# A conv-and-attention block on one core: its front, its third weight chunk and its last 512 columns rearranged

## The chip, the cores and the metric

The kernel runs on 1 core of one Trainium2 chip. The metric is device time in microseconds (us). Before the change the median of 3 runs was 740.27 us (739.8 to 740.4). The engines: TensorE (PE in the profile, its weight loads PEld), VectorE (DVE), ScalarE (ACT), GpSimd (POOL, all but unused here) and SyncE (SP), whose queue issues every transfer of this kernel before the change.

## The reference, cut to what matters

One layer over x (512 tokens by 1024), with a condition vector c for x and a vector c_ctx for 256 context tokens:

```python
sh, sc, gt = split(silu(c) @ w_mod + b_mod, 3)             # condition, 3 x 1024
h  = rmsnorm(x, pre_g) * (1 + sc) + sh                     # 512 x 1024
hc = rmsnorm(ctx, pre_g) * (1 + sc_c) + sh_c               # the same for the context, from c_ctx
parts = split(h @ w_in, IN_SIZES)                          # 10 parts of 1024 columns
attn  = neighbourhood_attention(rope(q), rope(k), v, k_ctx, v_ctx, rpb)
y_a = (silu(z_a) * b_gate * dwconv3(c_gate * x_in)) @ w_out_conv
y_b = (silu(z_b) * attn) @ w_out_attn
y   = (sigmoid(g_a) * y_a + sigmoid(g_b) * y_b) @ w_o
out = x + gt * rmsnorm(y, post_g)
```

## The kernel before, in words

Every large product is made in float32 accuracy out of reduced-precision halves: an operand is split into H (a cast on ScalarE, L70 or L287) and L (the rest, a subtraction on VectorE, L71 or L291), and a product is H·H + H·L + L·H, three passes. The weights come in chunks of 256 columns (two raw tiles of 512 KB each); `Chunks` loads one chunk ahead of the one in use, into two buffers `w` that alternate, with two raw buffers.

*The front.* SP issues the row of c, the small parameters `sp`, the four tiles of x (128 tokens each), then slabs. A slab `wm` holds the weights of the condition for 128 features; slab 8+k gives the scale of feature tile k, slab k the shift. `condition` (L259) multiplies a slab by silu(c), held in `cb` on all 128 partitions, and sums along the row on VectorE. silu(c) gets onto the partitions in this way: ScalarE takes Silu of the one row `crow`, TensorE multiplies it with a column of ones (L331), VectorE copies the two results to `cb` (L346). x is normalised tile by tile: the sum of squares (x0 and x2 on ScalarE, L341; x1 and x3 on VectorE, L337), a root on ScalarE (L342), a reciprocal and a scaling on VectorE (L343, L344), in the order of the tiles. Then TensorE transposes the four tiles, feature tile by feature tile (`turn_x`, L296).

Eight times, for feature tile k: `cast_first` and `rest_first` split the weights `fraw` of the first three chunks (768 columns), two conditions and a product with the gain (L356) make scale and shift, ScalarE modulates the transposed tile into `m` (L362), `split` gives `hx[0][k]`, `hx[1][k]` (named h0 to h7 below), and `steps(k)` adds 18 products of 512 columns into six accumulators (L303, L304 for twelve, L307 for six). Slabs and weights for k+3 are loaded in the turn of k; at k = 5 chunk three is loaded and split (`chunk.load(3)`). Behind the loop come the loads and norms of the context (the transfer of c_ctx, L372, reaches all 128 partitions: every partition reads the same 4 KB row), then the convolution of the first accumulators, and from there the list of chunks.

All of this stands inside `manual_schedule`: on TensorE, VectorE, ScalarE and SP the order is the order in which the code is written. What comes behind is put between by a scheduler where it finds room; in the kernel before it puts two groups of three products of chunk three (L108 to L110) between the steps 5, 6 and 7.

*The end.* y is made in two halves of 512 columns (c = 0, 1), and four token tiles t in each. For c = 1 the last tile's path is: 24 products of 512 columns (8 features by 3 passes, L703 to L705), a sum of squares on ScalarE (L715), a product with gpost on VectorE (L716), root (L723) and reciprocal (L724), four times y·r + x on 256 columns (L728), and a transfer behind each of them, on SP (L731):

```python
n = 512 if t < 3 else 256
for i in range(0, D, n):
    hs = slice(i, i + n)
    nc.vector.scalar_tensor_tensor(
        out=ys[t][:, hs], in0=ys[t][:, hs], scalar=r, in1=xr[t][:, hs], op0=ALU.mult, op1=ALU.add
    )
    nc.sync.dma_start(out[t * P:(t + 1) * P, hs], ys[t][:, hs])
```

Of the kernel before, what the change touches and what calls it, by code (L numbers as in the profile page):

```python
# [27 lines left out]
def layer(ctx: ExitStack, tc, xp, ctxt, cc, wmod, small, wfirst, win, wout, wo, rel, tab, out):  # L28
# [8 lines left out]
    class Banks:  # L37


        def __init__(self, *tags):  # L40
            self.tags, self.n = tags, 0
# [25 lines left out]
    def split(H, L, src, scale=None):  # L67

        if scale is None:
            nc.scalar.copy(H, src)  # L70
            nc.vector.tensor_sub(L, src, H.bitcast(F32))  # L71
        else:
            nc.scalar.mul(H, src, scale)
            nc.vector.scalar_tensor_tensor(
                out=L, in0=src, scalar=scale, in1=H.bitcast(F32), op0=ALU.mult, op1=ALU.subtract
            )

    def load_chunk(src):

        both = wp.tile([P, KT, 2, 256], F32R, name="w", bufs=2)  # L80
        H, L = both[:, :, 0], both[:, :, 1]
        for i in range(2):
            s = slice(4 * i, 4 * i + 4)
            raw = wp.tile([P, 4, 256], F32, name="raw", bufs=2)
            nc.sync.dma_start(raw, src[:, s])
            split(H[:, s], L[:, s], raw)
        return H, L, both

    class Chunks:

# [135 lines left out]
    with ExitStack() as p0:  # L226
# [3 lines left out]
        def load_x(src, i, n, tag, pool, bufs=1):  # L230
            xt = pool.tile([P, D], F32, name=n, tag=tag, bufs=bufs)
            nc.sync.dma_start(xt, src[i * P:(i + 1) * P])
            return xt
# [36 lines left out]
        ones = const.tile([1, P], F32, name="ones")  # L270
        bsc1 = const.tile([P, KT], F32, name="bsc1")
        crow = hp.tile([1, 2, S], F32, name="crow", tag="a0")
# [16 lines left out]
        def rest_first(k):  # L289
            H, L = first[k]  # L290
            nc.vector.tensor_sub(L, raws[k], H.bitcast(F32))  # L291
# [17 lines left out]

        E = mybir.EngineType  # L310
        with tc.manual_schedule(engines={E.PE, E.DVE, E.Activation, E.SP}):
            nc.sync.dma_start(crow, cc[0:1].rearrange("o (a n) -> o a n", a=2))
# [7 lines left out]
            nc.vector.memset(ones, 1.0)  # L320
            nc.vector.tensor_scalar(out=bsc1, in0=sp[:, BM + 8:BM + 16], scalar1=1.0, scalar2=None, op0=ALU.add)
            nc.vector.tensor_scalar(out=hcv, in0=sp[:, CW:CW + 32], scalar1=0.5, scalar2=None, op0=ALU.mult)


            nc.scalar.activation(crow, crow, AF.Silu)
            nc.scalar.activation(const.tile([1, 1], F32, name="dummy"), crow[:, 0, 0:1], AF.Square)
            nc.scalar.activation(const.tile([P, 1], F32, name="dummy2"), eps, AF.Sqrt)
            spread = []
            for i in range(2):
                spread.append(tps())  # L330
                nc.tensor.matmul(spread[i], lhsT=ones, rhs=crow[:, i], start=True, stop=True)  # L331
            junk_a = hp.tile([P, D], F32, name="junka", tag="a1")
            for i in range(4):
                top = tops[:, i:i + 1]
                if i % 2:
                    junk = st.tile([P, D], F32, name="junk")
                    nc.vector.tensor_tensor_reduce(  # L337
                        out=junk, in0=xn[i], in1=xn[i], scale=1.0, scalar=0.0, op0=ALU.mult, op1=ALU.add, accum_out=top
                    )
                else:  # L340
                    nc.scalar.activation(junk_a, xn[i], AF.Square, accum_out=top)  # L341
                nc.scalar.activation(top, top, AF.Sqrt, bias=eps, scale=1.0 / D)  # L342
                nc.vector.reciprocal(top, top)  # L343
                nc.vector.tensor_scalar(out=xn[i], in0=xn[i], scalar1=top, scalar2=None, op0=ALU.mult)  # L344
                if i < 2:
                    nc.vector.tensor_copy(cb[:, 0, i * S:(i + 1) * S], spread[i])  # L346
            turned_x = {k: turn_x(k) for k in range(2)}
# [24 lines left out]
            nc.sync.dma_start(cb[:, 1], cc[1:2].broadcast_to([P, D]))  # L372
            nc.scalar.activation(cb[:, 1], cb[:, 1], AF.Silu)
# [321 lines left out]
    for c in range(2):  # L695
        H, L = wos[c]
        cs = slice(c * S, (c + 1) * S)
        ps = [pj() for t in range(4)]

        def steps(t, ks):  # L700
            ts = slice(t * P, (t + 1) * P)
            for k in ks:
                nc.tensor.matmul(ps[t], lhsT=mm[0][k][:, ts], rhs=H[k], start=k == 0, stop=False)  # L703
                nc.tensor.matmul(ps[t], lhsT=mm[0][k][:, ts], rhs=L[k], start=False, stop=False)  # L704
                nc.tensor.matmul(ps[t], lhsT=mm[1][k][:, ts], rhs=H[k], start=False, stop=k == KT - 1)  # L705

        if c == 0:
            for t in range(4):
                nc.sync.dma_start(xr[t], xp[t * P:(t + 1) * P])

            for t in range(4):
                steps(t, range(KT - 1))
        for t in range(4):
            steps(t, range(KT - 1, KT) if c == 0 else range(KT))
            nc.scalar.activation(sq, ps[t], AF.Square, accum_out=sums[:, t, c:c + 1])  # L715
            nc.vector.tensor_mul(ys[t][:, cs], ps[t], gpost[:, cs])  # L716
            if c == 0:
                nc.vector.tensor_scalar(
                    out=sums[:, t, 2:3], in0=sums[:, t, 0:1], scalar1=1.0 / D, scalar2=EPS, op0=ALU.mult, op1=ALU.add
                )  # L720
            else:
                r = sums[:, t, 1:2]
                nc.scalar.activation(r, r, AF.Sqrt, bias=sums[:, t, 2:3], scale=1.0 / D)  # L723
                nc.vector.reciprocal(r, r)  # L724
                n = 512 if t < 3 else 256
                for i in range(0, D, n):
                    hs = slice(i, i + n)
                    nc.vector.scalar_tensor_tensor(  # L728
                        out=ys[t][:, hs], in0=ys[t][:, hs], scalar=r, in1=xr[t][:, hs], op0=ALU.mult, op1=ALU.add
                    )  # L730
                    nc.sync.dma_start(out[t * P:(t + 1) * P, hs], ys[t][:, hs])  # L731


# [80 lines left out]
```

## Time and profile before

| | |
|---|---|
| median of 3 runs | 740.27 us |
| the profiled execution's own time | 740.06 us |
| its span, from the first to the last instruction | 738.3 us |
| mean granted TensorE clock | 0.997 |
| busy: TensorE | 717.7 us, 97% |
| busy: VectorE | 516.9 us, 70% |
| busy: ScalarE | 333.9 us, 45% |
| chain that ended last, by engine | TensorE 93%, VectorE 3%, DMA 1%, ScalarE 1%, issue 1% |

A row of a timeline has the start in us, the duration, the engine, the line of the code, the operation, the tiles (out<-in), the shapes and the count of instructions that it stands for; a bracket at its end tells the idle time before it and what ended that. A row of the chain has start, duration, engine, tile, line. A row on a transfer has the tile, the queue, the count, the size and the time from issue to landing. A row of windows has the stretch, its length and sum with the count of instructions of PE, PEld, DVE, ACT, POOL, then granted clock, DMA share and GB/s; the first pair is PE's. PE's matmuls overlap: from the start of one to the start of the next (the pitch) is what one costs.

### The profile page before, as it was taken

What the parts mean: (1) busy time and instruction counts of PE and PEld (TensorE: products, weight loads), DVE (VectorE), ACT (ScalarE), POOL (GpSimd) and SP (SyncE); (2) the same over time, 40 slices, a digit from 0 to 9 for tenths busy, and PEclk for the clock granted to TensorE, in tenths of its full rate; (3) what the DMA queues carried; (4) which work ended last, traced back from release to release, by engine and by line L of the source; (5) the groups of instructions that cost most, each with busy time, mean ns of one, the idle gap of its engine ahead of it and who ended that gap; (6) DMA issues with size and microseconds to landing.
All of it is one profiled execution on the core that took longest, in us unless ns stands there. A gap on an engine that the chain in (4) does not pass through costs nothing.

```text
span 738.3 us, 9308 instructions
## 1 busy us (share of the span) xinstructions
PE 717.7 (97%) x3484; PEld 598.1 (81%) x3484; DVE 516.9 (70%) x1059; ACT 333.9 (45%) x615; POOL 0.7 (0%) x6
## 2 busy tenths in 40 slices
PE   3999999999999999999999999999999999999996
PEld 1788888878888888888888888888888888888885
DVE  6989997798797977968969779676763233234423
ACT  4565533464475644644636535445632223214321
POOL 0000000000000000000000000000000000000000
PEclk9999999999999999999999999999999999999998
DMA  8975883123211131221230321222132332234503
GB/s 333 378 281 177 278 292 115 58 71 115 72 51 62 46 129 59 72 71 64 87 108 18 93 91 62 82 78 95 58 114 70 102 114 83 89 115 145 197 4 111
DMA packets 25822, 85.57 MB, mean 116 GB/s; under 512 B 2993, under 2 KB 3505, under 8 KB 25778
## 3 DMA queue, kind: packets, MB, share of 16 engines
q1 hardware_dynamic: 25778, 84.99, 33.7%
q8 instruction: 27, 0.44, 0.2%
q14 instruction: 17, 0.14, 0.1%
HBM read 82.88 MB, written 2.10 MB: 115 GB/s over the span
## 4 chain that ended last, share of the span: by engine, by line
PE 93%; DVE 3%; DMA 1%; ACT 1%; issue 1%; SPq 0%; DVEq 0%; ACTq 0%
PE ps L110 20%; PE ps L109 20%; PE ps L108 20%; PE ps L121 6%; PE ps L551 4%; PE ps L536 4%; PE ps L125 3%; PE ps L505 3%; PE ps L704 2%; PE ps L703 2%; PE ps L705 2%; PE ps L303 2%; PE ps L304 2%; PE ps L133 2%; PE ps L307 1%; DMA fraw<-in_wfirst 1%
## 5 line engine op out<-in xcount | busy, mean ns | idle before, releaser
L108 PE MATMUL ps<-h,w 128*128 128x512 f32 x528 | 209.5, 397 | 0.0
L109 PE MATMUL ps<-h,w 128*128 128x512 f32 x528 | 206.2, 391 | 0.0
L110 PE MATMUL ps<-h,w 128*128 128x512 f32 x528 | 206.1, 390 | 0.0
L71 DVE TENSOR_TENSOR w<-raw,w 128x1024 fp32r<-128x1024 f32 (+1 forms) x98 | 113.5, 1175 | 60.7 <-ACT w L70 60.2
L70 ACT CAST w<-raw 128x1024 fp32r<-128x1024 f32 (+1 forms) x98 | 97.1, 1016 | 81.7 <-PE ps L110 63.2
L110 PEld LDWEIGHTS ps<-h,w 128*128 128x128 f32 x528 | 99.1, 188 | 21.0
L109 PEld LDWEIGHTS ps<-h,w 128*128 128x128 f32 x528 | 99.3, 188 | 19.3
L108 PEld LDWEIGHTS ps<-h,w 128*128 128x128 f32 x528 | 99.2, 188 | 19.4
L528 ACT ACTIVATE pt<-ps,m 128x512 f32<-128x512 f32 x64 | 44.2, 691 | 36.8 <-DVE m L525 35.7
L521 DVE CUSTOM_DVE_ANT_1 ps<-ps,bt 128x512 f32<-128x512 f32 x56 | 38.9, 697 | 17.0 <-PE ps L505 13.7
L71 DVE TENSOR_TENSOR TL<-ps,TH 128x512 fp32r<-128x512 f32 x64 | 43.6, 683 | 5.4 <-ACT TH L70 4.5
L121 PE MATMUL ps<-w,h 128*128 128x512 f32 x128 | 46.1, 402 | 0.0
L70 ACT CAST TH<-ps 128x512 fp32r<-128x512 f32 x64 | 37.2, 586 | 18.0 <-PE ps L536 17.7
L536 PE MATMUL ps<-ident,pt 128*128 128x128 f32 x256 | 38.2, 272 | 0.0
L664 DVE SCALAR_TENSOR_TENSOR g<-g,ps 128x512 f32<-128x512 f32 x16 | 11.0, 687 | 38.8 <-PE ps L110 38.8
L584 ACT ACTIVATE g<-ps 128x512 f32<-128x512 f32 x16 | 9.6, 598 | 60.2 <-PE ps L110 60.2
L536 PEld LDWEIGHTS ps<-ident,pt 128*128 128x128 f32 x256 | 31.1, 140 | 6.2 <-DVE pt L530 0.2
L125 PE MATMUL ps<-w,h 128*128 128x256 f32 x128 | 36.0, 281 | 0.0
L530 DVE TENSOR_SCALAR pt<-pt,z 128x512 f32<-128x512 f32 x64 | 30.9, 484 | 1.1
L121 PEld LDWEIGHTS ps<-w,h 128*128 128x128 f32 x128 | 24.1, 188 | 5.6
L470 ACT ACTIVATE qd<-ta 64x512 fp32r<-64x512 f32 x32 | 20.2, 631 | 18.5 <-PE ps L514 10.8
L551 PE MATMUL ps<-TH,V 128*128 128x256 f32 (+1 forms) x96 | 28.5, 319 | 0.0
(159 smaller groups left out, 1217.3 us busy)
## 6 DMA issues: line engine op xcount, KB each, us to landing
raw<-in_win SPq DMA_DIRECT2D x74, 512.0 KB, 4.0
wm<-in_wmod SPq DMA_DIRECT2D x34, 512.0 KB, 5.2
raw<-in_wout SPq DMA_DIRECT2D x16, 512.0 KB, 4.1
bt<-in_rel SPq DMA_DIRECT2D x16, 256.0 KB, 2.6
raw<-in_wo SPq DMA_DIRECT2D x8, 512.0 KB, 5.1
fraw<-in_wfirst SPq DMA_DIRECT2D x8, 384.0 KB, 5.3
x<-in_xp SPq DMA_DIRECT2D x4, 512.0 KB, 5.2
xr<-in_xp SPq DMA_DIRECT2D x4, 512.0 KB, 6.7
```

Source lines behind the costliest of these rows:

```text
L70: nc.scalar.copy(H, src)
L71: nc.vector.tensor_sub(L, src, H.bitcast(F32))
L108: nc.tensor.matmul(ps, lhsT=H[:, k, cs], rhs=mH[k], start=k == 0, stop=False)
L109: nc.tensor.matmul(ps, lhsT=H[:, k, cs], rhs=mL[k], start=False, stop=False)
L110: nc.tensor.matmul(ps, lhsT=L[:, k, cs], rhs=mH[k], start=False, stop=k == KT - 1)
L121: nc.tensor.matmul(ps, lhsT=mH[k][:, ts], rhs=both[:, k].rearrange("p a c -> p (a c)"), start=k == 0, stop=False, skip_group_check=True,)
L125: nc.tensor.matmul(ps[:, :256], lhsT=mL[k][:, ts], rhs=H[:, k], start=False, stop=k == KT - 1, skip_group_check=True)
L521: nc.vector.tensor_tensor_reduce(out=s3, in0=s3, in1=bt[:, e::4 - e][:, 0:2], scale=1.0, scalar=-3.0e38, op0=ALU.add, op1=ALU.max, accum_o ...
L528: nc.scalar.activation(pt, s, AF.Exp, bias=m, scale=1.0, accum_out=z)
L530: nc.vector.tensor_scalar(out=pt, in0=pt, scalar1=z, scalar2=None, op0=ALU.mult)
L536: nc.tensor.transpose(tp[:, c], pt[:, c * P:(c + 1) * P], ident)
L551: nc.tensor.matmul(o3[:, dst], lhsT=V[p][:, kt, h], rhs=src(t), start=n == 0 and t is TH, stop=n == len(work) - 1 and t is TL,)
```

## The change

Four things are done.

1. *Condition by transfer.* `crow`, the ones, the two products and the two copies are gone. The row of c is transferred to all 128 partitions of `cb` (512 KB) as the first transfer on SP, ahead of x; `sp` stands behind x. Silu runs on the whole of `cb` (128x1024).
2. *Shared norms.* x0 and x1 are squared on VectorE, x2 and x3 on ScalarE; x3 is scaled on ScalarE; the root of x1 stands behind the square of x2 on ScalarE. `rest_first(0)` moves behind the first two conditions.
3. *Unread products.* The transposes of feature tiles 0 and 1 go token tile by token tile, and between them `keep_busy` issues products of `cb` with the identity into `acc[5]` which nothing reads (2560 columns in all). `acc[5]` is started anew by step 0.
4. *Chunk three and the end.* Chunk three's transfers are issued at k = 5 as before, but its two splits stand behind the loop. The last tile of c = 1 is made in two halves of 256 columns, each with its own squares and product with gpost; the squares of the first half are joined into the bias of the root; y·r + x goes in pieces of 384, 384 and 256 columns, the middle piece's transfer is on ScalarE's queue.

```diff
+    class Chunk:
+        def __init__(self, src):
+            self.raws = [wp.tile([P, 4, 256], F32, name="raw", bufs=2) for _ in range(2)]
+            for i, raw in enumerate(self.raws):
+                nc.sync.dma_start(raw, src[:, 4 * i:4 * i + 4])
+        def split(self):
+            both = wp.tile([P, KT, 2, 256], F32R, name="w", bufs=2)
+            for i, raw in enumerate(self.raws):
+                s = slice(4 * i, 4 * i + 4)
+                split(both[:, s, 0], both[:, s, 1], raw)
+            return both[:, :, 0], both[:, :, 1], both
     def load_chunk(src):
+        return Chunk(src).split()
...
-            nc.sync.dma_start(crow, cc[0:1].rearrange("o (a n) -> o a n", a=2))
+            nc.sync.dma_start(cb[:, 0], cc[0:1].broadcast_to([P, D]))
+            xn = [load_x(xp, i, f"x{i}", f"u{i}", hp) for i in range(4)]
             nc.sync.dma_start(sp, small)
-            xn = [load_x(xp, i, f"x{i}", f"u{i}", hp) for i in range(4)]
...
+            nc.scalar.activation(cb[:, 0], cb[:, 0], AF.Silu)
...
-                if i % 2:
+                if i < 2:
...
+            def norm(i):
+                top = tops[:, i:i + 1]
                 nc.vector.reciprocal(top, top)
+                if i < 3:
+                    nc.vector.tensor_scalar(out=xn[i], in0=xn[i], scalar1=top, scalar2=None, op0=ALU.mult)
+                else:
+                    nc.scalar.mul(xn[i], xn[i], top)
+            def keep_busy(n, cols):
+                for _ in range(n):
+                    nc.tensor.matmul(acc[5][:, :cols], lhsT=ident, rhs=cb[:, 0, :cols], start=True, stop=True)
...
+            square(0)
+            square(1)
+            root(0)
+            norm(0)
+            square(2)
+            root(1)
+            root(2)
+            norm(1)
+            norm(2)
+            square(3)
+            root(3)
+            norm(3)
...
+            keep_busy(2, S)
+            turned_x = {k: tps() for k in range(2)}
+            for t in range(4):
+                for k in range(2):
+                    nc.tensor.transpose(turned_x[k][:, t * P:(t + 1) * P], xn[t][:, k * P:(k + 1) * P], ident)
+                keep_busy(1, 256 if t < 3 else S)
+            keep_busy(1, 256)
...
                 if k == 0:
-                    rest_first(k)
                     condition(k, 0, [0])
...
-                if k:
-                    rest_first(k)
+                rest_first(k)
...
                 elif k == 5:
-                    chunk.load(3)
+                    after = Chunk(order[3])
                 steps(k)
...
+            chunk.ahead[3] = after.split()
...
+        def evacuate(t, ps, cols, total):
+            nc.scalar.activation(sq[:, :ps.shape[-1]], ps, AF.Square, accum_out=total)
+            nc.vector.tensor_mul(ys[t][:, cols], ps, gpost[:, cols])
...
+                for i in range(2):
+                    qs, q = slice(256 * i, 256 * (i + 1)), (ps[t] if i == 0 else pj())[:, :256]
+                    steps(t, range(KT), q, qs)
+                    evacuate(t, q, slice(S + 256 * i, S + 256 * (i + 1)), (whole, r)[i])
+                    if i == 0:
+                        nc.vector.scalar_tensor_tensor(
+                            out=part, in0=whole, scalar=1.0 / D, in1=part, op0=ALU.mult, op1=ALU.add
+                        )
+            nc.scalar.activation(r, r, AF.Sqrt, bias=part, scale=1.0 / D)
+            nc.vector.reciprocal(r, r)
+            for n, (a, b) in enumerate(((0, 512), (512, 1024)) if t < 3 else ((0, 384), (384, 768), (768, 1024))):
...
+                (nc.scalar if t == 3 and n == 1 else nc.sync).dma_start(out[t * P:(t + 1) * P, a:b], ys[t][:, a:b])
```

In the rows below a line number, an operation, the tiles and the shape stand for one instruction each (x2: two alike); ISA is the multiply and sum of a condition or a square, and the short row behind it reads its sum. VectorE ahead of the first conditions, before (x_121 to x_125 are x1 to x3):

```order
L343 RECIPROCAL tops<-tops 128x1
L344 TENSOR_SCALAR x_121<-x_121,tops 128x1024
L346 COPY cb<-ps 128x512
L343 RECIPROCAL tops<-tops 128x1
L344 TENSOR_SCALAR x_123<-x_123,tops 128x1024
L337 ISA junk,tops<-x_125 128x1024
L337 ISA tops 128x1
L343 RECIPROCAL tops<-tops 128x1
L344 TENSOR_SCALAR x_125<-x_125,tops 128x1024
L291 TENSOR_TENSOR fL<-fraw,fH 128x768
L259 ISA junk,col_193<-wm,cb,bsc_101 128x1024
L259 ISA col_193 128x1
```

And after, where x_118 and x_120 are x1 and x2:

```order
L348 TENSOR_SCALAR x_118<-x_118,tops 128x1024
L346 RECIPROCAL tops<-tops 128x1
L348 TENSOR_SCALAR x_120<-x_120,tops 128x1024
L346 RECIPROCAL tops<-tops 128x1
L369 TENSOR_SCALAR bsc_100<-sp 128x8
L370 TENSOR_SCALAR hcv<-sp 128x32
L266 ISA junk,col_188<-wm,cb,bsc_100 128x1024
L266 ISA col_188 128x1
L266 ISA junk,col_188<-wm,cb,sp 128x1024
L266 ISA col_188 128x1
L385 TENSOR_TENSOR col_188<-col_188,sp 128x1
L296 TENSOR_TENSOR fL<-fraw,fH 128x768
```

The square of x3, a scaling and the copy to `cb` have left VectorE's queue, and fL (the low half of step 0's weights) has moved from ahead of the two conditions to behind them.

TensorE from its first instruction to the first product of step 0 (`ident` is the identity: a transpose; ps_ with its number is an accumulator or a transposed tile), before:

```order
L331 MATMUL ps_154<-crow_102,ones_100 128x512
L331 MATMUL ps_156<-crow_102,ones_100 128x512
L296 MATMUL ps_179<-ident_71,x0_119 128x128
L296 MATMUL ps_179<-ident_71,x1_121 128x128
L296 MATMUL ps_179<-ident_71,x2_123 128x128
L296 MATMUL ps_179<-ident_71,x3_125 128x128
L296 MATMUL ps_184<-ident_71,x0_119 128x128
L296 MATMUL ps_184<-ident_71,x1_121 128x128
L296 MATMUL ps_184<-ident_71,x2_123 128x128
L296 MATMUL ps_184<-ident_71,x3_125 128x128
L303 MATMUL ps_109<-h0_80,fH_189 128x512
```

And after, from behind the two transposes of x0 (two unread products of 512 columns stand ahead of those):

```order
L355 MATMUL ps_112<-cb_99,ident_71 128x256
L375 MATMUL ps_170<-ident_71,x1_118 128x128
L375 MATMUL ps_171<-ident_71,x1_118 128x128
L355 MATMUL ps_112<-cb_99,ident_71 128x256
L375 MATMUL ps_170<-ident_71,x2_120 128x128
L375 MATMUL ps_171<-ident_71,x2_120 128x128
L355 MATMUL ps_112<-cb_99,ident_71 128x256
L375 MATMUL ps_170<-ident_71,x3_122 128x128
L375 MATMUL ps_171<-ident_71,x3_122 128x128
L355 MATMUL ps_112<-cb_99,ident_71 128x512
L355 MATMUL ps_112<-cb_99,ident_71 128x256
L308 MATMUL ps_107<-h0_80,fH_185 128x512
```

The products with the ones are replaced by products with `cb`, and the transposes are now in four pairs, with an unread product behind each pair.

VectorE from the low half of h6 to that of h7 (`w` with `raw`: the low halves of a chunk), before, where w_546 is chunk four, and chunk three has its rows still further ahead:

```order
L71 TENSOR_TENSOR h6_86<-m_463,h6_86 128x512
L259 ISA junk_488,col0_460<-wm_380,cb_99,sp_70 128x1024
L259 ISA col0_460 128x1
L356 TENSOR_TENSOR col0_460<-col0_460,sp_70 128x1
L291 TENSOR_TENSOR fL_486<-fraw_382,fH_485 128x768
L71 TENSOR_TENSOR w_546<-raw_547,w_546 128x4x256
L71 TENSOR_TENSOR w_546<-raw_551,w_546 128x4x256
L71 TENSOR_TENSOR h7_87<-m_492,h7_87 128x512
```

And after, where w_505 is chunk three:

```order
L71 TENSOR_TENSOR h6_86<-m_454,h6_86 128x512
L266 ISA junk_479,col0_451<-wm_376,cb_99,sp_70 128x1024
L266 ISA col0_451 128x1
L385 TENSOR_TENSOR col0_451<-col0_451,sp_70 128x1
L296 TENSOR_TENSOR fL_477<-fraw_378,fH_476 128x768
L71 TENSOR_TENSOR h7_87<-m_483,h7_87 128x512
L71 TENSOR_TENSOR w_505<-raw_417,w_505 128x4x256
L71 TENSOR_TENSOR w_505<-raw_418,w_505 128x4x256
```

Both chunks' low halves stood ahead of the low half of h7; now chunk three's stand behind it, and chunk four's further on, behind a convolution.

More of the change, by code (lines that the diff above doesn't have):

```diff
@@ L319, in layer, with square @@
             nc.vector.memset(eps, EPS)
[L320 to L331, printed above, removed]
+            nc.scalar.activation(cb[:, 0], cb[:, 0], AF.Silu)
+            nc.scalar.activation(const.tile([P, 1], F32, name="dummy"), eps, AF.Sqrt)
             junk_a = hp.tile([P, D], F32, name="junka", tag="a1")
-            for i in range(4):
+            def square(i):
                 top = tops[:, i:i + 1]
-                if i % 2:
+                if i < 2:
                     junk = st.tile([P, D], F32, name="junk")
@@ L341, in layer, with root @@
                     nc.scalar.activation(junk_a, xn[i], AF.Square, accum_out=top)
+            def root(i):
+                top = tops[:, i:i + 1]
                 nc.scalar.activation(top, top, AF.Sqrt, bias=eps, scale=1.0 / D)
+            def norm(i):
+                top = tops[:, i:i + 1]
                 nc.vector.reciprocal(top, top)
[L344 to L347, printed above, removed]
+                if i < 3:
[17 more added lines that the diff above has]
+            norm(3)
+            nc.vector.tensor_scalar(out=bsc1, in0=sp[:, BM + 8:BM + 16], scalar1=1.0, scalar2=None, op0=ALU.add)
+            nc.vector.tensor_scalar(out=hcv, in0=sp[:, CW:CW + 32], scalar1=0.5, scalar2=None, op0=ALU.mult)
+            keep_busy(2, S)
[5 more added lines that the diff above has]
+            keep_busy(1, 256)
             for k in range(KT):
@@ L711, in layer @@
             for t in range(4):
-                steps(t, range(KT - 1))
+                steps(t, range(KT - 1), ps[t], slice(0, S))
         for t in range(4):
-            steps(t, range(KT - 1, KT) if c == 0 else range(KT))
-            nc.scalar.activation(sq, ps[t], AF.Square, accum_out=sums[:, t, c:c + 1])
-            nc.vector.tensor_mul(ys[t][:, cs], ps[t], gpost[:, cs])
+            part, whole, r = (sums[:, t, i:i + 1] for i in (2, 0, 1))
             if c == 0:
-                nc.vector.tensor_scalar(
-                    out=sums[:, t, 2:3], in0=sums[:, t, 0:1], scalar1=1.0 / D, scalar2=EPS, op0=ALU.mult, op1=ALU.add
-                )
[L721 to L731, printed above, removed]
@@ new lines, in layer @@
+                steps(t, range(KT - 1, KT), ps[t], slice(0, S))
+                evacuate(t, ps[t], cs, whole)
+                nc.vector.tensor_scalar(out=part, in0=whole, scalar1=1.0 / D, scalar2=EPS, op0=ALU.mult, op1=ALU.add)
+                continue
+            if t < 3:
+                steps(t, range(KT), ps[t], slice(0, S))
+                evacuate(t, ps[t], cs, r)
+            else:
+                for i in range(2):
[5 more added lines that the diff above has]
+                            out=part, in0=whole, scalar=1.0 / D, in1=part, op0=ALU.mult, op1=ALU.add
+                        )
```

20 lines of the change are left out of this document (6 added, 14 removed).

## The prediction

> **What bounds the kernel now.** I read the page first, then the chain of waits, then the timeline of the first 30 us and of the last 10, then the landings of single transfers.
>
> ```profile
> span 738.3 us, 9308 instructions
> PE 717.7 (97%) x3484; PEld 598.1 (81%) x3484; DVE 516.9 (70%) x1059; ACT 333.9 (45%) x615; POOL 0.7 (0%) x6
> ...
> PEclk9999999999999999999999999999999999999998
> ```
>
> TensorE is busy for 717.7 of 738.3 us. So only three things can move the time: when TensorE starts, how fast its first products go, and what follows its last one. The chain of waits gives the start:
>
> ```profile
> 0.74 0.35 SPq L312
> ...
> 15.37 1.28 DVE junk L259
> ...
> 19.64 0.79 PE ps L303
> 20.43 0.43 PE ps L304
> ```
>
> The first real product stands at 19.64. The work that leads to it is fixed: two conditions on VectorE from 15.37, the modulation, a cast, 4.27 us in all (19.64 - 15.37). What keeps the first condition until 15.37 is VectorE's own queue (timeline of VectorE):
>
> ```profile
> 9.62 0.16 DVE L343 RECIPROCAL tops<-tops 128x1 f32<-128x1 f32 x1 [0.36 <-ACT tops L342]
> ...
> 10.49 0.68 DVE L346 COPY cb<-ps 128x512 f32<-128x512 f32 x1
> ...
> 14.49 0.96 DVE L291 TENSOR_TENSOR fL<-fraw,fH 128x768 fp32r<-128x768 f32 x1
> ```
>
> It does two of the four squares, all four reciprocals and scalings, two copies of the condition and then the low part fL, all ahead of that condition. The next view is TensorE's timeline:
>
> ```profile
> 3.47 3.77 PE L331 MATMUL ps<-crow,ones 1*128 1x512 f32 x4 [3.47 <-ACT crow L325]
> ...
> 26.37 0.48 PE L303 MATMUL ps<-h,fH 128*128 128x512 f32 x1
> ...
> 30.95 0.48 PE L303 MATMUL ps<-h,fH 128*128 128x512 f32 x1
> ```
>
> The products of step 0 go at 0.43 each; step 0 takes 26.37 - 19.64 = 6.73 us, step 1, with the same work, 30.95 - 26.37 = 4.58. Step 1 is 18 products and four transposes, so a product goes at about 0.227 there. A slow first stretch costs 2.15 us. The row of the granted clock (PEclk, 9 in every early slice) doesn't show it; the pitch does.
>
> **The change, part by part.**
>
> *Condition by transfer.* It puts 512 KB at the head of SP's queue, which starts at 0.74, where x started at 1.55. Landings from the issue, for the first and last x tile and the slab behind them:
>
> ```profile
> x<-in_xp SPq DMA_DIRECT2D x1, 512.0 KB, 3.4
> x<-in_xp SPq DMA_DIRECT2D x1, 512.0 KB, 7.1
> wm<-in_wmod SPq DMA_DIRECT2D x1, 512.0 KB, 7.9
> ```
>
> The issues stand on SP's own timeline; of a row with a count it is the first:
>
> ```profile
> 1.55 1.84 SPq L232 DMA_DIRECT2D x<-in_xp  x4
> 3.43 0.92 SPq L249 DMA_DIRECT2D wm<-in_wmod  x2
> ```
>
> x3 is issued at 1.55 + 3 x 0.47 = 2.96 and lands at 10.06, the slab at 3.43 + 7.9 = 11.33: 1.27 per 512 KB, which is the queue's pace. The n-th transfer now is the one that was number n-1, and all go 0.81 earlier. cb lands at 0.74 + 3.4 = 4.1; x2 takes x3's place, 10.06 - 0.81 = 9.25. Everything behind lands 1.27 - 0.81 = 0.46 later; the first slab at 11.8, before it is wanted.
>
> *Shared norms.* The squares of x2 and x3 are ScalarE's now, with these prices:
>
> ```profile
> 9.49 1.04 ACT L341 ACTIVATE junka<-x 128x1024 f32<-128x1024 f32 x1
> 10.44 0.19 ACT L341 ACTIVATION_READ_ACCUMULATOR junka<-x 128x1 f32 x1
> 10.66 0.29 ACT L342 ACTIVATE tops<-tops,eps 128x1 f32<-128x1 f32 x1
> 54.60 1.06 ACT L373 ACTIVATE cb<-cb 128x1024 f32<-128x1024 f32 x1
> ```
>
> In ScalarE's new order the roots of x1 and x2 stand behind the square of x2. From its landing at 9.25: square and read to 10.45, first root to 10.75, then on VectorE two reciprocals with scalings, 0.87 each (9.62 to 10.49), to 12.55, the third reciprocal 0.2, bsc1 and hcv 0.2: the first condition starts at 12.95. The two copies are gone, fL(0) stands behind the conditions, and x3's scaling on ScalarE (12.8 to 13.85) lies beside them. First product: 12.95 + 4.27 = **17.2**, 2.4 earlier. Bounds: if the tiles land at 1.27 each from cb's 4.1, x2 is there at 7.9 and the product starts at 15.9; if the earlier issue brings nothing, x2 lands at 10.06 and it starts at 18.0. I take 17.2, because the fourth landing is a row and the smooth pace is not.
>
> *Unread products.* 2560 columns; the ones-products took 3.77 us for 1024, so 9.4 us slow, half if fast. They start at about 5.2 (4.1 and Silu's 1.06). The first two end by 9.0, the last ones wait for x3's transposes at 13.9. They lie in time in which TensorE has nothing to do, up to 17.2. If the array stayed slow throughout, the row from x1 on (four pairs of transposes less one at 0.44, products of 256, 256, 512 and 256 columns, 4.7 us) would run from 11.7 to 17.7 and hold step 0 by 0.5. What they buy isn't shown in any row. Bounds: nothing (step 0 slow, 6.73), or all 2.15. I take all: in before the slow pitch ended 4.6 us after a dense start, and here TensorE has two such stretches, 5.2 to 10 and 11.7 to 15.6, with 1.6 us idle ahead of step 0.
>
> [...]
>
> Step 1 then starts at 17.2 + 4.58 = 21.8, where it was 26.37: **4.57 us earlier**. Its input is ready: behind the first gain product VectorE has fL 0.88 (14.49 to 15.37), a condition 1.28, the low part 0.69 (53.95 below), a condition 1.28; with modulation and cast 21.4. Only 0.4 is in hand.
>
> *Chunk three.* This gives TensorE nothing by itself:
>
> ```profile
> 49.20 0.48 PE L108 MATMUL ps<-h,w 128*128 128x512 f32 x1
> ...
> 51.56 2.47 DVE L71 TENSOR_TENSOR w<-raw,w 128x1024 fp32r<-128x1024 f32 x2
> ...
> 53.95 0.69 DVE L71 TENSOR_TENSOR h<-m,h 128x512 fp32r<-128x512 f32 x1
> ...
> 55.70 1.28 DVE L259 CUSTOM_DVE_ANT_0 junk<-wm,cb,bsc 128x1024 f32<-128x1024 f32 x1 [1.06 <-ACT cb L373]
> ```
>
> In before the splits stand in the way of h6 and h7, but TensorE fills the time with products of chunk three (L108 at 49.20), which have to be done anyway. Afterwards steps 1 to 5 end at 21.8 + 5 x 4.58 = 44.7, steps 6 and 7 (18 products of 0.227) at 52.9; the last low part is done at about 46.8, chunk three's halves (2.47) at 49.3, 3.6 before they are read. Chunk four's halves, which were in the loop, now fall behind it, into this stretch:
>
> ```profile
> 60.00:120.00 60.00, 60.00 (x279) 49.31 (x278) 58.99 (x102) 27.38 (x45) 0.00 (x0) 1.00 0.69 228
> 98.57 1.22 DVE L71 TENSOR_TENSOR w<-raw,w 128x1024 fp32r<-128x1024 f32 x1
> 103.74 0.39 PE L110 MATMUL ps<-h,w 128*128 128x512 f32 x1
> ```
>
> VectorE is busy for 58.99 of 60 us there. The tightest place is chunk seven: its first low half ends at 99.79, its first reader starts at 103.74, 3.95 in hand. VectorE enters the stretch at 50.7 (Silu of cb: casts to 48.3, table and Silu 2.35) where it was 55.70, 5.0 earlier, but with 2.47 more to do: 2.5 earlier against TensorE's 4.57. That takes 2.0 of the 3.95. No wait, if nothing else slips.
>
> *Closing 512 columns in two.* Two halves of 256 cost TensorE, the others gain:
>
> ```profile
> 175.35 1.86 PE ps L551 x12
> 731.37 0.39 PE L705 MATMUL ps<-w,mg 128*128 128x512 f32 x1
> 731.79 0.60 ACT L715 ACTIVATE sq<-ps 128x512 f32<-128x512 f32 x1 [4.42 <-PE ps L705]
> 732.51 0.69 DVE L716 TENSOR_TENSOR ys<-ps,gpost 128x512 f32<-128x512 f32 x1 [3.23 <-ACT sq L715]
> 733.31 1.67 DVE L728 SCALAR_TENSOR_TENSOR ys<-ys,sums,xr 128x256 f32<-128x256 f32 x4
> 733.82 1.79 SPq L731 DMA_DIRECT2D out_x<-ys  x4
> L143 ACT COPY ta<-ps 128x256 f32<-128x256 f32 x32 | 11.9, 372 | 32.8 <-PE ps L125 19.0 <-PE ps L137 9.9 <-DVE tb L437 2.8
> L144 DVE TENSOR_TENSOR ta<-ta,ps 128x256 f32<-128x256 f32 x32 | 12.9, 415 | 12.9 <-ACT ta L143 12.9
> ```
>
> L551's twelve are four of 512 and eight of 256 columns: (1.86 - 4 x 0.227) / 8 = 0.119. 48 x 0.119 - 24 x 0.227 = +0.26. Behind the last product, half the width: its own end about -0.1, the square 0.60 to 0.37, -0.23, the product with gpost 0.69 to 0.42, -0.27. Three pieces of 384, 384, 256 for four of 256: 0.53 + 0.53 + 0.48 (384 taken between 256's 0.40 and some 0.67 for 512) for 1.67, -0.13. The four issues on SP came 0.47 apart, slower than the pieces, so the last stood at 735.22, 0.24 behind its piece; three on two queues don't queue, -0.2. Sum -0.67. An issue on ScalarE's queue has no row, so between -0.2 and -0.8; I take -0.6.
>
> **Sum.** 4.57 + 0.6 = 5.2. The profiled execution took 740.06 (span 738.3 and 1.8 around it): 734.9. The median of the runs is 740.27, 0.2 above: **735.1 us**.
>
> **Rivals.** *The array is slow at step 0* (the gaps around the transposes, or the 1.6 us, let it fall back): step 0 takes 6.73 from 17.2 to 17.7, the gain at step 1 is 1.95 to 2.45, with the closing 2.5 to 3.0: 737.2 to 737.7. For it: in before the transposes at 8 to 15 ran slow although ones-products had filled 3.47 to 7.24. Against it: those products had one row, these have 128.
>
> *VectorE doesn't follow.* If more than 1.9 us slip in its full stretch (a scheduled step that now waits for the context transposes, say), TensorE waits at chunk seven for the excess. All of the front would be lost if VectorE came to chunk seven at its old time, 99.8 against 99.2 wanted, with 3.95 spent: then the change does nothing but the closing, 739.5. An excess of 1 us gives 736.
>
> *Slower than before: the broadcast.* All 128 partitions read one 4 KB row. If that takes long, x lands later one for one. The gain is gone once cb takes 1.27 + 5.2 = 6.5 us, and 9 us give 742.8. Before has the same transfer once, in a full queue:
>
> ```profile
> 38.11 1.08 SPq L232 DMA_DIRECT2D c<-in_ctxt  x2
> 43.23 1.05 ACT L70 CAST w<-raw 128x1024 fp32r<-128x1024 f32 x1 [0.23 <-DMA raw<-in_win]
> c<-in_ctxt SPq DMA_DIRECT2D x1, 512.0 KB, 7.9
> ```
>
> The raw tile ahead of it had landed at 43.2, c0 behind it at 46.0: 2.8 us for cb and c0, 1.5 for cb. So this is unlikely.
>
> **Chances.** The sum 0.63, with its own range 733.6 (tiles at the smooth pace) to 736.5 (x2 at 10.06, or the 0.4 at step 1 lost); slow array 0.19; VectorE late by 1 to 3 us 0.08, by all of it 0.06; broadcast 0.04. The range over these reaches from 733.5 to 737.8. A measurement of this kernel tells about 0.2% (1.5 us) from no change: faster 0.9, within 0.06, slower 0.04.
>
> **What would show it.** The first reader of h0 at 17.2 (15.9 to 18.0) and 0.227 between its products; step 1 at 21.8; cb landed near 4.1; no TensorE wait between 21 and 140, above all none at chunk seven; the span's end 6.2 to 6.3 us behind the last product's start, where it was 6.9. Wrong I'd be if step 0's products stand 0.43 apart, or if x2 lands after 10.1.

## The result, and the profile after

The median went from 740.14 us (4 runs, 739.8 to 740.4) to 734.72 us (4 runs, 734.68 to 737.3), a ratio of 0.9938 with a 95% interval of 0.9926 to 0.9951 (the medians alone give 0.9927). The profiled execution of the changed kernel is the 737.3: its span is 733.0, like the 732.9 of the three others, and only what lies around the span was longer. So the traces are compared by their spans: 738.3 and 733.0, 5.3 us apart.

The page after, its first two lines:

```profile
span 733.0 us, 9376 instructions
PE 717.9 (98%) x3518; PEld 598.9 (82%) x3518; DVE 513.7 (70%) x1056; ACT 335.1 (46%) x617; POOL 0.7 (0%) x6
```

TensorE is as busy as before (717.9 after 717.7), but that figure now holds the unread products as well, so it does not tell where the time went: the timelines do. The chain after, from the first issue to step 0 (start, duration, what):

```profile
0.74 0.38 SPq L317
...
2.12 6.91 DMA x<-in_xp
...
9.05 1.15 ACT junka L338 x2
...
12.45 0.61 DVE junk L266
...
16.68 0.50 PE ps L308
```

The landing of x2, its square on ScalarE, the norms, the two conditions: that is the path the forecast took. TensorE's timeline after:

```profile
6.41 3.75 PE L355 MATMUL ps<-cb,ident 128*128 128x512 f32 x4 [6.41 <-ACT cb L326]
...
13.81 1.46 PE L355 MATMUL ps<-cb,ident 128*128 128x512 f32 x4
16.68 0.50 PE L308 MATMUL ps<-h,fH 128*128 128x512 f32 x1 [1.41 <-ACT h L70]
...
21.29 0.48 PE L308 MATMUL ps<-h,fH 128*128 128x512 f32 x1
```

The first unread products go slowly (3.75 us for two of 512 columns), the last ones fast (1.46 for 768 columns), and step 0 follows fast after 1.41 us of nothing: 21.29 - 16.68 = 4.61. The end of before (ScalarE's squares of tile 2; that of tile 3 stands in the prediction), and the end of after (squares of tile 2 and of the second half of tile 3, then VectorE and the issues):

```profile
726.35 0.60 ACT L715 ACTIVATE sq<-ps 128x512 f32<-128x512 f32 x1 [4.42 <-PE ps L705]
```

```profile
721.40 0.60 ACT L738 ACTIVATE sq<-ps 128x512 f32<-128x512 f32 x1 [4.42 <-PE ps L733]
...
727.21 0.38 ACT L738 ACTIVATE sq<-ps 128x256 f32<-128x256 f32 x1 [2.46 <-PE ps L733]
...
727.71 0.42 DVE L739 TENSOR_TENSOR ys<-ps,gpost 128x256 f32<-128x256 f32 x1 [2.44 <-ACT sq L738]
...
728.24 1.54 DVE L770 SCALAR_TENSOR_TENSOR ys<-ys,sums,xr 128x384 f32<-128x384 f32 x3
728.89 1.25 SPq L773 DMA_DIRECT2D out_x<-ys  x2
729.42 0.37 ACTq L773 DMA_DIRECT2D out_x<-ys  x1
```

From these rows the 5.3 us come apart without a rest. It is one execution of each kernel; how far two fronts of one code can differ is seen below.

| stretch | before | after | difference |
|---|---|---|---|
| to the first product of step 0 | 19.64 | 16.68 | -2.96 |
| step 0 | 6.73 | 4.61 | -2.12 |
| step 1 to the square of tile 2 | 699.98 | 700.11 | +0.13 |
| square of tile 2 to the last square | 5.44 | 5.81 | +0.37 |
| last square to the end of the span | 6.51 | 5.79 | -0.72 |

What was not expected stands in the middle of the kernel. VectorE waits 2.59 us for the first context tile, where before it had no wait, and at chunk seven (the `w` row is its first low half, the PE row the first reader of that) it is later against TensorE than forecast:

```profile
74.31 0.42 DVE L71 TENSOR_TENSOR hc<-ctT,hc 128x256 fp32r<-128x256 f32 x1 [2.59 <-ACT hc L70]
...
96.71 1.21 DVE L71 TENSOR_TENSOR w<-raw,w 128x1024 fp32r<-128x1024 f32 x1
98.73 0.39 PE L117 MATMUL ps<-h,w 128*128 128x512 f32 x1
```

The half is ready at 97.92, its reader starts at 98.73: 0.8 us in hand, where before had 3.95 (the reader's weight load starts 0.2 earlier still, at 98.51). No TensorE time is lost, but nearly all of the slack is.

### The profile page after: what moved, and what is told of

Read it like the earlier page. It is cut to its first block, busy times and chain, and to the rows that moved or that the text cites. A ratio compares the mean times of both kernels' runs of the same rounds, so it can differ in the third digit from the quotient of the medians.

```text
span 733.0 us, 9376 instructions
## 1 busy us (share of the span) xinstructions
PE 717.9 (98%) x3518; PEld 598.9 (82%) x3518; DVE 513.7 (70%) x1056; ACT 335.1 (46%) x617; POOL 0.7 (0%) x6
## 4 chain that ended last, share of the span: by engine, by line
PE 94%; DVE 2%; DMA 1%; ACT 1%; issue 1%; SPq 0%; DVEq 0%; ACTq 0%
PE ps L115 20%; PE ps L116 20%; PE ps L117 20%; PE ps L128 6%; PE ps L733 6%; PE ps L580 4%; PE ps L565 4%; PE ps L132 3%; PE ps L534 3%; PE ps L308 2%; PE ps L140 2%; PE ps L309 2%; PE ps L312 1%; PE ps L543 1%; DMA x<-in_xp 1%; PE ps L144 1%
```

## Experiments

The theory to be tested: the order of the norms makes the first product earlier, the unread products make step 0 fast, the late split of chunk three lets both through, and the closing is worth less than 0.6. Each kernel was timed against the kernel before on its chip; a time below is a median, and its ratio is to before.

**The closing alone.** The kernel before with the last tile in two halves, as in the diff's last part.

> The kernel before with the closing 512 columns in two halves as the only change. Theory (the two traces at that place): 0.37 us more between the square of tile 2 and the last square (5.81 instead of 5.44), 0.75 us less from the last square to the end of the span (5.75 instead of 6.50): the span 0.4 shorter, 737.9, and about 739.8 us. Rival (the forecast's terms): 0.6, 739.5 us. Rival: nothing is left of it, 740.1 us. First product and step 1 stay at 19.6 and 26.4.

739.26 us against 740.25, ratio 0.9987 (0.9978 to 0.9996). The interval holds 0.3 to 1.6 us, so the time rules out the third and cannot tell the first two apart. The trace is finer: from the square of tile 2 (725.86) to the end of the span (737.5) are 11.64 us, in before 11.95 (726.35 to 738.3): 0.3, as in the changed kernel (0.37 - 0.72 = -0.35). The rest of the span's 0.8 is an earlier step 1 in this execution (25.87), in a front that nobody had touched. Fronts of one code thus differ by half a us between executions.

**No unread products.**

```diff
-            keep_busy(2, S)
...
-                keep_busy(1, 256 if t < 3 else S)
-            keep_busy(1, 256)
```

> The changed kernel without its seven unread products. Theory A (they bring the array to its full rate): first product still at 16.7, step 0 at 0.43 a product and 6.7 us long, step 1 at 23.4 instead of 21.3: 2.1 us more, 736.8 us. Theory B (the full rate comes from elsewhere, the transposes in pairs or the time since the start): step 0 at 0.23, 734.7 us as the changed kernel.

736.49 us, 0.9952 (0.9939 to 0.9964): theory A. TensorE's timeline of this kernel:

```profile
13.43 0.69 PE L374 MATMUL ps<-ident,x 128*128 128x128 f32 x2 [0.57 <-ACT x L350]
16.58 0.80 PE L308 MATMUL ps<-h,fH 128*128 128x512 f32 x1 [2.46 <-ACT h L70]
17.17 0.63 PE L309 MATMUL ps<-h,fL 128*128 128x512 f32 x1
...
20.59 0.40 PE L309 MATMUL ps<-h,fL 128*128 128x512 f32 x1
20.82 0.40 PE L308 MATMUL ps<-h,fH 128*128 128x512 f32 x1
...
23.01 0.48 PE L308 MATMUL ps<-h,fH 128*128 128x512 f32 x1
```

The first product stands where it stood, but products go at 0.43 until 20.6 (a row's 0.63 is its length, not its pitch), and step 1 comes at 23.01. The unread products are worth 1.7 to 1.8 us here: step 0 takes 6.43 us without them, less than the 6.73 of the kernel before.

**Transposes in their place.**

```diff
-                    nc.tensor.matmul(acc[5][:, :cols], lhsT=ident, rhs=cb[:, 0, :cols], start=True, stop=True)
+                    for c in range(0, cols, P):
+                        for _ in range(2):
+                            nc.tensor.transpose(acc[5][:, c:c + P], cb[:, 0, c:c + P], ident)
```

> The changed kernel with each unread product replaced by unread transposes that take the array about as long (two of 128 columns for every 128 columns). Theory A (any dense work of the array raises its rate): step 0 at 0.23, 734.7 us. [...]

734.71 us, 0.9926 (0.9913 to 0.9938): theory A, as fast as with products. Its timeline:

```profile
6.31 3.65 PE L357 MATMUL ps<-ident,cb 128*128 128x128 f32 x16 [6.31 <-ACT cb L326]
...
16.58 0.50 PE L308 MATMUL ps<-h,fH 128*128 128x512 f32 x1 [1.39 <-ACT h L70]
...
21.16 0.48 PE L308 MATMUL ps<-h,fH 128*128 128x512 f32 x1
```

Sixteen transposes first take 0.23 each; step 0 is fast (4.58), with nothing but transposes ahead of it. So float32 transposes of 128x128 are followed by the full rate here as the products are (4.61). In the kernel before there are eight, at 8.26, 10.63, 12.09 and (five) from 14.54, after 1.02, 1.92, 0.98 and 1.98 us of nothing, and step 0 behind them was slow (6.73): what differs here is how many there are and how densely they come, not what they are.

**Chunk three split in the loop.**

```diff
-                    after = Chunk(order[3])
+                    chunk.load(3)
...
-            chunk.ahead[3] = after.split()
```

> The changed kernel with chunk three split in the loop at k = 5 again, as before the change. Theory A (the late split lets the front's gain through, since chunk three lands at 41 to 42.5 us whatever the front does): h6 waits for the splits of chunk three, step 6 starts at 47.4 instead of 44.2, two groups of chunk three's products fill 1.4 us of it, step 7 waits some 0.7 us more: 2.5 to 3.2 us more, about 737.5 us. Theory B (the forecast's step, that it gives TensorE nothing by itself): 734.7 us.

739.42 us, 0.9992 (0.9983 to 1.0001): theory A, and more than it said. ScalarE, VectorE and TensorE of this kernel, a fence each:

```profile
41.25 1.05 ACT L70 CAST w<-raw 128x1024 fp32r<-128x1024 f32 x1 [4.63 <-DMA raw<-in_win]
...
46.22 0.78 ACT L390 ACTIVATE m<-ps,col 128x512 f32<-128x512 f32 x1 [1.90 <-DVE col L385]
```

```profile
42.33 2.51 DVE L71 TENSOR_TENSOR w<-raw,w 128x1024 fp32r<-128x1024 f32 x2 [4.86 <-ACT w L70]
44.77 1.28 DVE L266 CUSTOM_DVE_ANT_0 junk<-wm,cb,sp 128x1024 f32<-128x1024 f32 x1
```

```profile
47.05 0.50 PE L115 MATMUL ps<-h,w 128*128 128x512 f32 x1 [2.76 <-ACT m L390]
47.70 0.50 PE L308 MATMUL ps<-h,fH 128*128 128x512 f32 x1
...
52.47 0.50 PE L308 MATMUL ps<-h,fH 128*128 128x512 f32 x1 [0.41 <-ACT h L70]
```

The cast of chunk three waits for a transfer that lands at 41.2. Its issue is 3.8 us earlier than in the kernel before (32.12 for 35.94), its landing only 0.7 (41.2 for 41.9), since it takes 9.1 us instead of 6.0: the DMA engines are full all the time from 30 us on (mean busy share 1.03, as in the changed kernel from 30 to 42 us; before, 0.92 there). So the front's gain doesn't move it. Behind that cast in ScalarE's and VectorE's queues stands what h6 needs. Step 6 starts at 47.70 where the changed kernel has 44.16, step 7 ends 4.21 later, and with 0.15 more behind it the square of tile 2 comes 4.36 later (725.76 for 721.40). Only one product of chunk three went into the gap, where I had counted on two groups. So the front's 5 us reach the end only with the split moved: without it all the rest of the change gives 0.8 us (740.25 to 739.42, and the interval still holds no gain at all), the closing's 0.35 among them. The late split alone, in the kernel before, was not run.

**Which unread products.** With the first two alone (the lines of the loop and the one behind it taken out), and with all but the first two:

> The changed kernel with only the first two unread products (512 columns each, from 6.4 to 10.2), none between or behind the transposes. Theory A (the rate falls back while the array is mostly idle from 11 to 16.6): step 0 slow for about 4 us as without any, 736.5 us. Theory B (one early dense stretch is enough): step 0 at 0.23 a product, 734.7 us.

> The changed kernel with only the unread products between and behind the transposes, from 10.4 on, without the first two. Theory A (about 4 us of dense work bring the full rate, and the pairs and products from 10 to 15 are as much): step 0 at 0.23 from its first or second product, 734.7 us, at most 735.2. Theory B (the stretch from 6.4 is needed too): step 0 slow for most of 4 us, 736.5 us.

736.3 us, 0.9948 (0.9934 to 0.9961), and 734.66 us, 0.9924 (0.9911 to 0.9936): theory A in both. The transposes and the first product, with the first two alone:

```profile
9.96 0.44 PE L375 MATMUL ps<-ident,x 128*128 128x128 f32 x2
...
13.50 0.69 PE L375 MATMUL ps<-ident,x 128*128 128x128 f32 x2 [0.81 <-ACT x L350]
16.64 0.79 PE L308 MATMUL ps<-h,fH 128*128 128x512 f32 x1 [2.45 <-ACT h L70]
```

And with the late ones alone:

```profile
10.00 0.66 PE L374 MATMUL ps<-ident,x 128*128 128x128 f32 x2 [10.00 <-DVE x L348]
...
13.92 0.39 PE L374 MATMUL ps<-ident,x 128*128 128x128 f32 x2
...
16.56 0.50 PE L308 MATMUL ps<-h,fH 128*128 128x512 f32 x1 [0.96 <-ACT h L70]
```

A pair of transposes is the gauge: 0.44 long and less at the full rate, 0.66 to 0.69 at the slow one. The first kernel reaches the full rate at 10 and has lost it by 13.5; the second reaches it at 13.9, after 4 us of dense work, and keeps it. The first two products are not needed.

**None at the end.** Without the last two (512 and 256 columns):

> The changed kernel without the last two unread products (512 and 256 columns, from 13.8 to 15.3): the array is idle from 14.0 to 16.6, 2.6 us ahead of step 0 instead of 1.4. Theory A (such a gap brings the slow rate back): step 0 slow for up to 4 us, 735.5 to 736.5 us. Theory B (the rate lasts over 2.6 us): step 0 at 0.23 a product, 734.7 us.

736.55 us, 0.9951 (0.9937 to 0.9964): theory A.

```profile
13.85 0.44 PE L375 MATMUL ps<-ident,x 128*128 128x128 f32 x2 [0.24 <-ACT x L350]
16.99 0.80 PE L308 MATMUL ps<-h,fH 128*128 128x512 f32 x1 [2.70 <-ACT h L70]
...
24.25 0.48 PE L308 MATMUL ps<-h,fH 128*128 128x512 f32 x1
```

The rate is full at 13.85 and gone after 2.70 us without work; step 0 then takes 7.26 us. A gap of 1.41 us, in the changed kernel, left it. The profiled execution is the slowest of the five (737.7; the others 736.2 to 737.31) and has, with the one at 737.31, the lowest mean granted clock (0.993; the rest 0.995 to 0.997), so the slow stretch is likely among the longest here.

**The norms as before.** Square, root and norm tile by tile, x1 and x3 squared and all four scaled on VectorE:

```diff
-                if i < 2:
+                if i % 2:
...
-                if i < 3:
+                if i < 4:
...
+            for i in range(4):
+                square(i)
+                root(i)
+                norm(i)
```

> The changed kernel with the norms as before: x0 and x2 squared on ScalarE, x1 and x3 on VectorE, all four scaled on VectorE, square, root and norm tile by tile. Theory A (VectorE's queue sets the first product): norms one behind the other, first condition at about 16.7 instead of 12.4, first product at about 21, step 1 at 25.5: 4.2 us more, 738.9 us. Theory B (the landing of x2 and x3 sets it, the work is hidden): first product at 16.7 to 17.6, 734.7 to 735.6 us.

740.76 us, 1.0007 (0.9998 to 1.0016): as slow as before. VectorE's first condition and TensorE's first products in this kernel:

```profile
16.46 1.28 DVE L266 CUSTOM_DVE_ANT_0 junk<-wm,cb,bsc 128x1024 f32<-128x1024 f32 x1
```

```profile
20.74 0.80 PE L308 MATMUL ps<-h,fH 128*128 128x512 f32 x1 [1.08 <-ACT h L70]
...
27.13 0.48 PE L308 MATMUL ps<-h,fH 128*128 128x512 f32 x1
```

Theory A holds to 0.3 us at the first product (20.74 for 21), and what it left out is the rate: the waits between the norms thin out TensorE's work (the four scaled tiles are ready at 10.08, 12.53, 13.89 and 16.35, in the changed kernel at 9.97, 11.38, 12.23 and 13.49), step 0 is slow again (27.13 - 20.74 = 6.39), and the rest of the 6 us is that. It is VectorE's queue, not the landing of x, that had set the start: from 9.12 to the condition VectorE works for 6.07 of 7.34 us and waits for a root three times, 0.4 us each. Against the kernel before (19.64) the first product is even 1.1 us later: x0 is squared on ScalarE again, and there its square stands behind Silu of the broadcast `cb` and starts at 7.63, where it was 5.07. So the transfer of c does not pull the start forward; the order and sharing of the norms does, by 4.06 us (20.74 to 16.68), more than the 2.96 that the front gained as a whole.

**c as one row.** One row, two products with ones, copied to `cb` by ScalarE; one unread product of 512 columns less:

```diff
-            nc.sync.dma_start(cb[:, 0], cc[0:1].broadcast_to([P, D]))
+            nc.sync.dma_start(crow, cc[0:1].rearrange("o (a n) -> o a n", a=2))
...
+            for i in range(2):
+                nc.tensor.matmul(acc[i], lhsT=ones, rhs=crow[:, i], start=True, stop=True)
...
+                nc.scalar.copy(cb[:, 0, i * S:(i + 1) * S], acc[i])
```

> The changed kernel with c as one row again, spread by two products with ones, but copied to cb by ScalarE; one unread product of 512 columns less. Theory A (the 512 KB at the head of the queue hold x back): x2 lands at 8.4 instead of 9.05, first product 0.6 to 0.7 us earlier, at 16.0, 734.0 us. Theory B (the slabs or the weights of step 0 end last): 734.7 us. Theory C (the products with the ones and the copies hold a root or the transposes): 735 us or more.

734.35 us (733.66 to 734.45), 0.9917 (0.9903 to 0.993). ScalarE's square of x2, and TensorE's steps 0 and 1:

```profile
8.27 1.06 ACT L347 ACTIVATE junka<-x 128x1024 f32<-128x1024 f32 x1 [0.58 <-DMA x<-in_xp]
```

```profile
15.91 0.50 PE L310 MATMUL ps<-h,fH 128*128 128x512 f32 x1 [1.41 <-ACT h L70]
...
20.48 0.48 PE L310 MATMUL ps<-h,fH 128*128 128x512 f32 x1
```

Theory A in the trace: x2 is there 0.8 earlier, step 0 at 15.91. In time 0.37 us less than the changed kernel, all its runs below all of that kernel's, though the two were not timed side by side: half of what the trace promises (by the medians of the spans, 732.9 and 732.3, it is 0.6).

**The root of x1 first.** On ScalarE `root(1)` ahead of `square(2)`, in the changed kernel and in the one with c as one row:

> The changed kernel with the root of x1 ahead of the square of x2 on ScalarE, nothing else. Theory A (norm of x1 0.6 us earlier, then the slab of the shift, landed at 12.6, and the weights, cast by 14.9, end last): first product at 16.3 instead of 16.7, 734.35 us. Theory B (the square of x2 is held by the root and takes back what it gives): 734.7 us or 0.1 more.

> The kernel with c as one row (the experiment before) and, on ScalarE, the root of x1 ahead of the square of x2. Theory A (VectorE's wait of 1.7 us for that root, from 7.9 to 9.6, goes; then slab and weights of step 0 end last): first condition at 11.0, the cast of step 0's weights at 13.2 to 14.1, first product at 15.5 where it was 15.9: 0.4 us less than that kernel, 733.95 us. Theory B (what is gained in the front is lost again, because VectorE has nothing in hand at chunk seven): 734.35 us, with a TensorE wait near 97 us.

734.76 us, 0.9927 (0.9915 to 0.994): nothing is gained. ScalarE and VectorE in the first of them, a fence each:

```profile
9.10 0.29 ACT L342 ACTIVATE tops<-tops,eps 128x1 f32<-128x1 f32 x1 [1.12 <-DVE tops L334]
```

```profile
12.16 0.16 DVE L346 RECIPROCAL tops<-tops 128x1 f32<-128x1 f32 x1 [0.41 <-ACT tops L342]
...
12.43 1.28 DVE L266 CUSTOM_DVE_ANT_0 junk<-wm,cb,bsc 128x1024 f32<-128x1024 f32 x1
```

The reciprocal of x3 stands ahead of the condition in VectorE's queue and waits for its own root: the wait moved from x1 to x3, and the condition starts at 12.43 as before. Theory B has a part in that. The root of x1 waits for VectorE's square of x1 and holds the square of x2 on ScalarE (9.30 for 9.05), so x3's root starts at 11.83 where it was 11.64. With c as one row: 734.11 us (733.33 to 734.26), 0.9915 (0.9902 to 0.9929), first product at 16.07, not 15.5: the same wait for x3's root, in an execution in which x2 came 0.37 later, and no measurable difference from 734.35. No TensorE wait stands near 97 us, so its theory B has nothing for it. The two kernels with c as one row beat the kernel before and, by 0.4 and 0.6 us, the changed one.

**VectorE loaded.** Two unread products of 1024 columns on VectorE, behind its wait at 74 us:

```diff
+            if k == 1:
+                for _ in range(2):
+                    junk = st.tile([P, D], F32, name="junk")
+                    nc.vector.tensor_mul(junk, cb[:, 0], cb[:, 0])
             condition(k, 1)
```

> The changed kernel with two unread products of 128x1024 on VectorE (2.4 us) behind its wait for the first modulated context tile at 74 us. Theory A (VectorE has 0.8 us in hand at chunk seven, no more): TensorE waits about 1.6 us near 98 us, 736.3 us. Theory B (VectorE has as much in hand as the forecast said, 1.9 us): a wait of 0.5 us, 735.2 us. Theory C (it is hidden): 734.7 us, no wait.

736.17 us, 0.9947 (0.9934 to 0.9959): theory A. TensorE's weight loads at chunk seven:

```profile
100.19 0.19 PEld L117 LDWEIGHTS ps<-h,w 128*128 128x128 f32 x1 [1.32 <-DVE w L71]
```

It waits 1.32 us for the low half, and the time is 1.45 longer. Of the 2.44 us added about 1 was covered: the 0.8 in hand, and two products of another unit that the scheduler put ahead of the reader here (0.45), less what the reader's weight load needs first.

## Why the prediction was right, and where not

It said 735.1 us (733.5 to 737.8); 734.72 was measured.

- *Condition and norms:* first product 17.2 forecast, 16.68 measured. The landing of x2 was 9.03 for 9.25, and ScalarE's and VectorE's small steps overlap more than their lengths say (first condition 12.40 for 12.95). `cb` landed at 5.1, not 4.1. Silu and the unread products wait for it, but nothing on the path to step 0 does. The norms tile by tile show that VectorE's queue was the right thing to reckon.
- *Unread products:* all of the 2.15 us was taken, 2.12 came. That was a choice between bounds; the runs now show that the products among and behind the transposes bring 1.7 to 1.8 us of it. The rest lies in the slow stretch itself, which varies from execution to execution: step 0 took 6.73 us in the kernel before, 6.47 with the closing alone. The rival of a slow array was near: 1.3 us more of idle time before step 0, and it would have been the result (736.55).
- *Chunk three:* the reading of this step failed, though not the sum, which was made with the late split in place. "This gives TensorE nothing by itself" was read off the kernel before, where TensorE came late enough. With TensorE 5 us earlier, the chunk's transfer, which lands at 41.2 to 41.9 in either kernel, would have held 4.4 of them. The late split is a condition of the front's gain; what it gives without that gain stays open.
- *VectorE at chunk seven:* 1.95 us in hand forecast, 0.8 measured. TensorE reached its reader 5.01 earlier (103.74 to 98.73), and VectorE its half 1.86 earlier (98.57 to 96.71), not 2.5: ahead of it lies the 2.59 us wait for the first context tile, a slip as the rival named it, and 0.8 us short of costing time.
- *Closing:* 0.6 forecast, 0.35 measured. The terms from the last square on were about right (0.83 forecast, 0.72 measured); the products of 256 columns were priced too low. 48 of them took 5.81 us, 0.121 each; 0.119, from a row of twelve mixed products, and 0.1 for the end of the last one made the TensorE term 0.16 instead of 0.37.
- *Broadcast:* it cost more than thought at the head (4.4 us to landing) and x came behind it, but the whole price against one row is 0.4 us in time, 0.8 in the trace; far from the 5.2 that would have undone the gain.

So the sum was right partly by luck: the start was 0.5 better than forecast, the closing 0.25 worse, and the middle 0.13, which had stood at nothing.

## To carry to other kernels

When a start is pulled forward, look for what arrives at a fixed time, a transfer above all, and stands in an in-order queue ahead of the work that is now due: what was harmless before eats the gain (here chunk three, which landed at 41.2 to 41.9 in either kernel and, split in the loop, held 4.4 of 5 us). When a step of slow products stands behind a gap, work that nobody reads is worth trying there: here it brought 1.8 us (736.49 to 734.72), transposes as much as products (734.71). How near to the step it reached and how dense it was both counted in these runs: a gap of 1.41 us left step 0 fast, one of 2.70 made it slow, and with the norms as before the gap was only 1.08 us and step 0 was slow (6.39 us), with the tiles that the filling goes between ready over 6.3 us instead of 3.5. Slack is to be measured again after each gain: here one of 5 us left 0.8 of 3.95.

## What was not expected of the hardware

In these traces the array's rate shows in the granted clock only after it has been reached and lost. At the start it doesn't show: the kernel before is granted 1.00 up to 24 us, and only the pitch tells the rates apart, 0.43 or 0.227 a product of 512 columns. Where the rate had risen and fell again, the clock stands at 0.50, and the slow products lie in that stretch. One row of windows each for the kernel before, the one with none at the end and the one with the norms as before:

```profile
0.00:24.00 24.00, 10.87 (x22) 6.10 (x23) 16.69 (x34) 12.37 (x20) 0.70 (x6) 1.00 0.91 350
```

```profile
15.91:22.73 6.82, 5.74 (x14) 4.48 (x15) 6.82 (x12) 4.06 (x6) 0.00 (x0) 0.50 1.03 409
```

```profile
14.41:24.64 10.23, 7.84 (x17) 4.64 (x17) 9.80 (x20) 4.55 (x8) 0.00 (x0) 0.50 1.02 405
```

With the first two alone it is 0.50 from 13.23 to 20.05. So in these three the slow rate is a granted clock of 0.50; that the slow start is the same state is likely, since the pitch is the same, but the record of the clock does not show it.

The stretches at 0.50 last 6.82, 6.82 and 10.23 us; the third is 3.41 longer than the others, which is half of their length. In the 3.41 us ahead of each fall TensorE was busy for 1.46 to 1.75 us, and no idle stretch ahead of a fall was longer than 1.6. The changed kernel has as little work in the 3.41 us ahead of step 0 (1.73) and kept its rate, so the share alone does not decide. A gap of 1.41 us left the rate full, one of 2.70 lost it, 1.6 us after its start, and the slow stretch at step 0 then lasted from 3.4 us (the first two products alone) over 4.0 (none) and 4.6 (before) to 5.8 (none at the end). What decides when the rate rises and falls, these runs do not show.
